# Weight casts of a projection queued behind the decays of an mLSTM head on ScalarE, in a one-layer Fox and mLSTM mixer

## The chip, the cores and the metric

The kernel runs on one core of a Trainium2 chip. The metric is the time of one execution on the device in microseconds (us); the median of several executions stands for a kernel. All data and all arithmetic are 32-bit floats; on TensorE a product of two matrices is made as three matmuls, from each operand split into a high part and a low rest.

## The reference

One layer over 256 positions of width 2048: a first feed-forward network, a token mixer, a second feed-forward network, each behind an adaptive layer norm whose nine shift, scale and gate vectors are computed from a conditioning vector. The change lies in the mixer, which is cut here to what matters:

```python
z = h @ w_in                                   # 256 x 2048 @ 2048 x 6160
y_fox = _fox_attention(fq, fk, fv, fox_logf)   # 8 heads of 128
mq, mk = ...                                   # causal convolution and silu, 4 heads of 128
hm = _mlstm(mq, mk, mv, m_i, m_logf)           # 4 heads, values of 256
...
y = jnp.concatenate([y_fox, y_mlstm], axis=-1)
return y @ w_out
```

An mLSTM head is, in the kernel's closed form over all 256 positions, a matrix of products q k, weighted by a decay exp(-max(0, ...)) below the diagonal, times the values, divided by a bounded row sum.

## The kernel before, in words

Weights come from HBM in blocks of 1 MB (tile `raw`, three buffers, one DMA each on SP's queue). For each block `load_w` lets ScalarE make the high parts `hi` (two casts of 128x1024, L150) and VectorE the low rests `lo` (two subtractions, L151), six buffers each. TensorE then runs the three matmuls of `mm3` (L399 to L401): `hi` with the high input, `hi` with the low input, `lo` with the high input.

The projections for the Fox heads are made by `form_a_four`, four blocks of 512 rows each. In the order of the program they are named `fb` (queries of heads 4 to 7), `fbk` (their keys), `fa` and `fak` (heads 0 to 3); `fbk00` and `fbk01` are the two halves of block 0 of `fbk`, and so on. Each block is 48 matmuls. After each block `step()` does two things: it pumps rows of the conditioning projection (`ar`, 512 KB rows of `w_ada` with two buffers, added into `acc` by VectorE at L165), and it advances the side work, which is Python generators of heads.

An mLSTM head (`mlstm_head`) is such a generator. Its first part makes on TensorE the row of decays `gb` and the products `sps` and `gb`; on ScalarE a Relu (L1306) and an Exp (L1307) write the decays `dm`; VectorE masks them (L1308) and multiplies them with the products (L1309). `sps` has a single PSUM buffer (tag `m5`), so the products of the next head can be written only when L1309 has read those of this one. Its second part makes `nps` on TensorE (L1315 to L1317), the divisor `dn` on VectorE (L1320 to L1323), the quotient `yM` and its squares on ScalarE (L1324, L1325). The PSUM tiles `gb` and `nps` share three buffers (tag `aux`).

A scheduler sets the order on each engine when the program is built; every engine then runs its own queue strictly in that order and waits on semaphores. `tc.issue_after(ins)` adds no wait: it orders the instructions of its block behind `ins` on the engine of `ins`.

## Time and profile before

| what | us |
|---|---|
| median of 3 runs | 1928.33 |
| lowest and highest run | 1928.22, 1933.65 |
| the profiled execution's own time | 1927.28 |
| its span | 1925.6 |
| TensorE busy in it | 1891.5 |
| ScalarE busy in it | 953.7 |
| VectorE busy in it | 1483.4 |

The span is the time between the first and the last instruction of the profile; the 1.7 us between it and the execution's own time are start and end. TensorE's matmuls are pipelined, so its busy time says that it has work, not that it runs at its peak; its idle time and its granted clock are what can be won. PE is TensorE, DVE is VectorE, ACT is ScalarE, SP issues DMAs.

### The profile page before, as it was taken

How to read it: one execution, taken by the hardware profiler on the slowest of the kernel's cores; microseconds unless marked ns; L12 is line 12 of the kernel's file. 1: busy time of each engine (PE TensorE's matmuls, PEld its weight loads, DVE VectorE, ACT ScalarE, POOL GpSimd, SP SyncE). 2: the span in 40 equal slices, each digit the busy share in tenths (PEclk: the TensorE clock that was granted, in tenths of full speed). 3: DMA queues.
4: the chain of work that ended last, by engine and by line, in shares of the span. 5: the costliest groups of instructions: out<-in, count | busy, mean ns of one | idle time of the engine just before them, and what ended most of it. 6: DMA issues, size and time to landing. Idle time of an engine off the chain costs nothing.

```text
span 1925.6 us, 32413 instructions
## 1 busy us (share of the span) xinstructions
PE 1891.5 (98%) x13133; PEld 1724.6 (90%) x13133; DVE 1483.4 (77%) x1847; ACT 953.7 (50%) x1359; POOL 59.7 (3%) x88
## 2 busy tenths in 40 slices
PE   6999999999999999999999999999999999999997
PEld 3999999999988887699989886999999999988886
DVE  6788989877789898888988887867766655555776
ACT  3554454444454555845655645565444444444562
POOL 1111100000000000100000000000000000000000
PEclk9999999999999999999999999999999999999999
DMA  9978969999898787499988883987777766755552
GB/s 359 375 262 313 328 218 296 337 331 306 266 339 296 267 301 236 138 321 317 319 300 272 315 300 114 338 282 246 262 248 260 246 213 196 240 184 189 196 196 89
DMA packets 283662, 510.92 MB, mean 265 GB/s; under 512 B 10962, under 2 KB 134514, under 8 KB 282488
## 3 DMA queue, kind: packets, MB, share of 16 engines
q1 hardware_dynamic: 275640, 480.53, 73.4%
q0 software_dynamic: 7872, 28.32, 4.4%
q8 instruction: 103, 1.69, 0.4%
q14 instruction: 47, 0.39, 0.1%
HBM read 506.71 MB, written 2.10 MB: 264 GB/s over the span
## 4 chain that ended last, share of the span: by engine, by line
PE 84%; DVE 7%; DMA 5%; issue 2%; ACT 1%; SPq 0%; DVEq 0%; POOL 0%; ACTq 0%
PE gu_f L401 8%; PE gu_f L400 8%; PE gu_f L399 8%; PE o_f L399 6%; PE o_f L401 6%; PE o_f L400 6%; PE s L400 4%; PE s L399 4%; PE s L401 4%; DMA ar<-in_w_ada_dram 3%; PE fs L401 1%; PE fs L399 1%; PE fs L400 1%; PE o_mx L399 1%; PE o_mx L401 1%
## 5 line engine op out<-in xcount | busy, mean ns | idle before, releaser
L165 DVE SCALAR_TENSOR_TENSOR acc<-ar,csil,acc 128x1024 f32<-128x1024 f32 (+1 forms) x167 | 211.4, 1267 | 52.2 <-DMA ar<-in_w_ada_dram 51.5
L400 PE MATMUL s<-xlo_f,hi_s 128*128 128x256 f32 x768 | 213.6, 278 | 1.2 <-DVE xlo_f L331 1.2
L399 PE MATMUL s<-xhi_f,hi_s 128*128 128x256 f32 x768 | 213.4, 279 | 0.0
L401 PE MATMUL s<-xhi_f,lo_s 128*128 128x256 f32 x768 | 213.3, 278 | 0.0
L401 PE MATMUL gu_f<-xhi_f,lo_f2i 128*128 128x256 f32 x768 | 212.0, 276 | 0.0
L399 PE MATMUL gu_f<-xhi_f,hi_f2i 128*128 128x256 f32 x768 | 212.0, 276 | 0.0
L400 PE MATMUL gu_f<-xlo_f,hi_f2i 128*128 128x256 f32 x768 | 212.0, 276 | 0.0
L151 DVE TENSOR_TENSOR lo_f2i<-raw_f2i,hi_f2i 128x1024 fp32r<-128x1024 f32 x96 | 117.4, 1224 | 92.4 <-ACT hi_f2i L150 92.4
L401 PE MATMUL gu_f<-xhi_f,lo_f1i 128*128 128x256 f32 x640 | 176.7, 276 | 0.0
L399 PE MATMUL gu_f<-xhi_f,hi_f1i 128*128 128x256 f32 x640 | 176.7, 276 | 0.0
L400 PE MATMUL gu_f<-xlo_f,hi_f1i 128*128 128x256 f32 x640 | 176.7, 276 | 0.0
L150 ACT CAST hi_f2i<-raw_f2i 128x1024 fp32r<-128x1024 f32 x96 | 100.8, 1050 | 135.4 <-PE gu_f L400 124.6
L150 ACT CAST hi_s<-raw_s 128x1024 fp32r<-128x1024 f32 x96 | 100.6, 1052 | 130.3 <-PE s L400 93.4
L400 PEld LDWEIGHTS s<-xlo_f,hi_s 128*128 128x128 f32 x768 | 145.5, 189 | 1.5 <-DVE xlo_f L331 1.5
L401 PEld LDWEIGHTS s<-xhi_f,lo_s 128*128 128x128 f32 x768 | 145.4, 189 | 0.0
L399 PEld LDWEIGHTS s<-xhi_f,hi_s 128*128 128x128 f32 x768 | 144.9, 189 | 0.0
L399 PEld LDWEIGHTS gu_f<-xhi_f,hi_f2i 128*128 128x128 f32 x768 | 144.2, 188 | 0.2
L400 PEld LDWEIGHTS gu_f<-xlo_f,hi_f2i 128*128 128x128 f32 x768 | 144.2, 188 | 0.2
L401 PEld LDWEIGHTS gu_f<-xhi_f,lo_f2i 128*128 128x128 f32 x768 | 144.2, 188 | 0.0
L151 DVE TENSOR_TENSOR lo_f2o<-raw_f2o,hi_f2o 128x1024 fp32r<-128x1024 f32 x86 | 105.2, 1223 | 43.3 <-ACT hi_f2o L150 43.3
L165 DVE SCALAR_TENSOR_TENSOR gate<-ar,csil,gate 128x1024 f32<-128x1024 f32 (+1 forms) x94 | 117.5, 1251 | 25.4 <-DMA ar<-in_w_ada_dram 25.2
L151 DVE TENSOR_TENSOR lo_s<-raw_s,hi_s 128x1024 fp32r<-128x1024 f32 x96 | 115.5, 1219 | 27.4 <-ACT hi_s L150 27.2
(478 smaller groups left out, 5511.6 us busy)
## 6 DMA issues: line engine op xcount, KB each, us to landing
ar<-in_w_ada_dram SPq DMA_DIRECT2D x227, 512.0 KB, 5.4
raw_f2i<-in_ffn_w_in_dram SPq DMA_DIRECT2D x48, 1024.0 KB, 5.2
raw_s<-in_ffn_w_in_dram SPq DMA_DIRECT2D x47, 1024.0 KB, 7.6
raw_f1o<-in_ffn_w_out_dram SPq DMA_DIRECT2D x44, 1024.0 KB, 7.3
raw_f2o<-in_ffn_w_out_dram SPq DMA_DIRECT2D x44, 1024.0 KB, 5.1
raw_f1i<-in_ffn_w_in_dram SPq DMA_DIRECT2D x40, 1024.0 KB, 7.4
ar<-in_w_ada_dram POOLq DMA_DIRECT2D x48, 512.0 KB, 6.9
raw_mxo<-in_w_out_dram SPq DMA_DIRECT2D x16, 1024.0 KB, 6.0
```

The lines of the kernel that those rows point to most:

```text
L150: S.copy(hi, src)
L151: return V.tensor_tensor(out=lo, in0=src, in1=hi.bitcast(F32), op=ALU.subtract)
L165: V.scalar_tensor_tensor(out=acc, in0=raw, scalar=csil[:, k:k + 1], in1=acc, op0=ALU.mult, op1=ALU.add)
L399: PE.matmul(o, ah, bh, start=start, stop=False)
L400: PE.matmul(o, ah, bl, start=False, stop=False)
L401: PE.matmul(o, al, bh, start=False, stop=stop)
```

## The change

`mlstm_head` keeps its last Exp instruction in a two-place list `decays`. `form_a_four` hands the older place to `load_w` as `behind`, and shifts the list after each block and before its `step()`. So the two casts of a weight block are ordered on ScalarE behind the decays of the head whose first part was issued after the block two before. Head 0 is issued after block 2 of `fb`, head 1 after block 3 of `fb`, head 2 after block 0 of `fbk`, head 3 after block 2 of `fbk`; the blocks bound by the order are 0, 1 and 2 of `fbk` and 0 of `fa`. No instruction is added that computes anything, and TensorE's order stays as it was.

```diff
     emptied = [None]
+    decays = [None, None]
...
-            for k4, hi, lo in load_w(W[u * 512:(u + 1) * 512, c0:c0 + 512], 4, 512, f"{name}{u}"):
+            for k4, hi, lo in load_w(W[u * 512:(u + 1) * 512, c0:c0 + 512], 4, 512, f"{name}{u}",
+                                     behind=decays[0]):
...
+            decays[:] = decays[1], None
             step()
...
-            S.activation(d, d, AF.Exp, scale=-1.0)
+            decays[1] = S.activation(d, d, AF.Exp, scale=-1.0).ins
```

The scheduler places everything around these casts anew. The first place is ScalarE's queue (ACT) at head 0. `hi_fbk..` are the casts, `dm0` the decays of head 0, `qs4` a scaled copy of finished queries. Before:

```order
L150 CAST hi_fbk00_10448<-raw_fbk0_10446 128x1024
L150 CAST hi_fbk01_10476<-raw_fbk0_10446 128x1024
L150 CAST hi_fbk10_10540<-raw_fbk1_10538 128x1024
L150 CAST hi_fbk11_10568<-raw_fbk1_10538 128x1024
L1306 ACTIVATE dm0_10354<-gb0_10352,nacol_8749 128x256
L1306 ACTIVATE dm0_10354<-gb0_10352,nacol_8749 128x128
L1307 ACTIVATE dm0_10354<-dm0_10354 128x256
L1307 ACTIVATE dm0_10354<-dm0_10354 128x128
```

In the changed kernel, whose lines lie three further down, the same place reads:

```order
L1309 ACTIVATE dm0_10354<-gb0_10352,nacol_8749 128x256
L1309 ACTIVATE dm0_10354<-gb0_10352,nacol_8749 128x128
L1310 ACTIVATE dm0_10354<-dm0_10354 128x256
L1310 ACTIVATE dm0_10354<-dm0_10354 128x128
L150 CAST hi_fbk00_10448<-raw_fbk0_10446 128x1024
L150 CAST hi_fbk01_10476<-raw_fbk0_10446 128x1024
L1386 ACTIVATE qs4_10711<-pr_fb0_10121 128x256
```

The decays of head 0 stood behind four casts and now stand ahead of them; the casts of block 1 have moved further back, behind the decays of head 1.

The second place is VectorE's queue (DVE) from the same point on: `lo_fbk..` are the low rests, `acc` takes a row `ar` of the conditioning projection, `dg` and `scsh` finish one of its vectors. Before:

```order
L151 TENSOR_TENSOR lo_fbk00_10449<-raw_fbk0_10446,hi_fbk00_10448 128x1024
L165 SCALAR_TENSOR_TENSOR acc5_0_10041<-ar5_0_8_10427,csil_94,acc5_0_10041 128x1024
L151 TENSOR_TENSOR lo_fbk01_10477<-raw_fbk0_10446,hi_fbk01_10476 128x1024
L151 TENSOR_TENSOR lo_fbk10_10541<-raw_fbk1_10538,hi_fbk10_10540 128x1024
L195 TENSOR_TENSOR dg6_1_1_10335<-bc6_1_1_10332,ident_79 128x512
L151 TENSOR_TENSOR lo_fbk11_10569<-raw_fbk1_10538,hi_fbk11_10568 128x1024
L197 TENSOR_REDUCE scsh_103<-dg6_1_1_10335 128x4
L1308 TENSOR_TENSOR dm0_10354<-dm0_10354,trir_87 128x128
L199 TENSOR_TENSOR scsh_103<-scsh_103,bcol_98 128x2x4
L1308 TENSOR_TENSOR dm0_10354<-dm0_10354,trir_87 128x128
L1309 TENSOR_TENSOR dm0_10354<-sps0_10353,dm0_10354 128x256
L1309 TENSOR_TENSOR dm0_10354<-gb0_10352,dm0_10354 128x128
```

In the changed kernel:

```order
L165 SCALAR_TENSOR_TENSOR acc5_0_10041<-ar5_0_8_10427,csil_94,acc5_0_10041 128x1024
L195 TENSOR_TENSOR dg6_1_1_10335<-bc6_1_1_10332,ident_79 128x512
L197 TENSOR_REDUCE scsh_103<-dg6_1_1_10335 128x4
L199 TENSOR_TENSOR scsh_103<-scsh_103,bcol_98 128x2x4
L1311 TENSOR_TENSOR dm0_10354<-dm0_10354,trir_87 128x128 x2
L1312 TENSOR_TENSOR dm0_10354<-sps0_10353,dm0_10354 128x256
L1312 TENSOR_TENSOR dm0_10354<-gb0_10352,dm0_10354 128x128
L151 TENSOR_TENSOR lo_fbk00_10449<-raw_fbk0_10446,hi_fbk00_10448 128x1024
L151 TENSOR_TENSOR lo_fbk01_10477<-raw_fbk0_10446,hi_fbk01_10476 128x1024
```

The four low rests of blocks 0 and 1 have moved from ahead of head 0's products to behind them; the row `ar5_0_8` and the end of the conditioning vector stay ahead.

The third place is VectorE at the low rests of block 2 of `fbk`, with head 0's divisor `dn0.` and head 2's decays. Before:

```order
L165 SCALAR_TENSOR_TENSOR acc5_0_10041<-ar5_0_9_10504,csil_94,acc5_0_10041 128x1024
L151 TENSOR_TENSOR lo_fbk20_10622<-raw_fbk2_10619,hi_fbk20_10621 128x1024
L165 SCALAR_TENSOR_TENSOR acc5_0_10041<-ar5_0_10_10596,csil_94,acc5_0_10041 128x1024
L151 TENSOR_TENSOR lo_fbk21_10650<-raw_fbk2_10619,hi_fbk21_10649 128x1024
L1308 TENSOR_TENSOR dm1_10432<-dm1_10432,trir_87 128x128 x2
L1309 TENSOR_TENSOR dm1_10432<-sps1_10431,dm1_10432 128x256
L1309 TENSOR_TENSOR dm1_10432<-gb1_10430,dm1_10432 128x128
L165 SCALAR_TENSOR_TENSOR acc5_0_10041<-ar5_0_11_10599,csil_94,acc5_0_10041 128x1024
L151 TENSOR_TENSOR lo_fbk30_10722<-raw_fbk3_10719,hi_fbk30_10721 128x1024
L165 SCALAR_TENSOR_TENSOR acc5_0_10041<-ar5_0_12_10677,csil_94,acc5_0_10041 128x1024
L1320 SCALAR_TENSOR_TENSOR dn00_10512<-nps00_10507,em_8750 128x1
```

In the changed kernel:

```order
L165 SCALAR_TENSOR_TENSOR acc5_0_10041<-ar5_0_10_10596,csil_94,acc5_0_10041 128x1024
L165 SCALAR_TENSOR_TENSOR acc5_0_10041<-ar5_0_11_10599,csil_94,acc5_0_10041 128x1024
L1323 SCALAR_TENSOR_TENSOR dn00_10512<-nps00_10507,em_8750 128x1
L1323 SCALAR_TENSOR_TENSOR dn01_10518<-nps01_10508,em_8750 128x1
L1325 TENSOR_TENSOR dn00_10512<-nps00_10507,dn00_10512 128x1
L1325 TENSOR_TENSOR dn01_10518<-nps01_10508,dn01_10518 128x1
L1326 RECIPROCAL dn00_10512<-dn00_10512 128x1
L1326 RECIPROCAL dn01_10518<-dn01_10518 128x1
L1311 TENSOR_TENSOR dm2_10526<-dm2_10526,trir_87 128x128 x2
L1312 TENSOR_TENSOR dm2_10526<-sps2_10525,dm2_10526 128x256
L1312 TENSOR_TENSOR dm2_10526<-gb2_10524,dm2_10526 128x128
L151 TENSOR_TENSOR lo_fbk20_10622<-raw_fbk2_10619,hi_fbk20_10621 128x1024
```

The low rest of block 2 now follows the divisor of head 0 and the decays of head 2, and all of them follow row 11 of the conditioning projection. On ScalarE the quotients `yM0` and their squares stand ahead of head 2's Relu and Exp, and those ahead of the casts of block 2. On SP's queue the DMA of row 11 now stands ahead of that of block 0 of `fa`, and not behind it.

## Prediction

> **What bounds the kernel now.** I read the page first (busy shares), then TensorE's list of waits, then the stretches around the longest wait, then the timelines of the four queues there.

> ```profile
> PE 1891.5 (98%) x13133; PEld 1724.6 (90%) x13133; DVE 1483.4 (77%) x1847; ACT 953.7 (50%) x1359; POOL 59.7 (3%) x88
> PE sps L1303 <- DVE dm L1309: 4.1, 1, 4.1
> 800.00:900.00 100.00, 99.15 (x624) 88.52 (x623) 82.59 (x125) 59.14 (x105) 2.30 (x6) 1.00 0.92 317
> 970.00:980.00 10.00, 5.90 (x36) 5.65 (x35) 10.00 (x18) 4.19 (x9) 0.00 (x0) 0.83 0.97 337
> 980.00:990.00 10.00, 10.00 (x83) 9.75 (x81) 7.34 (x15) 5.89 (x15) 0.00 (x0) 1.00 0.93 318
> ```

> TensorE is the bound: it is busy 98% of the span. The second row is its wait (total, times, longest) that the change touches: the products of head 1 wait once, 4.1 us, for VectorE. The stretches give busy time by engine, then the granted clock: around the wait it falls to 0.83, ten us later it is 1.00. Time won there is won at the end, since TensorE stays the bound behind it.

> ```profile
> 963.83 0.59 PE L1303 MATMUL sps<-o 128*128 128x256 f32 x2
> 964.40 0.37 PE L399 MATMUL pr_fb<-xhi_mx,hi_fb 128*128 128x256 f32 x1
> 969.98 0.28 PE L1301 MATMUL gb<-ng,rowsel 128*128 128x256 f32 x1
> 974.36 0.70 PE L1303 MATMUL sps<-o 128*128 128x256 f32 x2 [4.10 <-DVE dm L1309]
> 982.22 1.03 PE L1315 MATMUL nps<-yM,dm 128*128 128x257 f32 x4
> 984.22 0.37 PE L399 MATMUL pr_fbk<-xhi_mx,hi_fbk 128*128 128x256 f32 x1
> 989.78 1.03 PE L1315 MATMUL nps<-yM,dm 128*128 128x257 f32 x4
> 990.89 0.47 PE L399 MATMUL pr_fbk<-xhi_mx,hi_fbk 128*128 128x256 f32 x1
> 996.56 1.03 PE L1315 MATMUL nps<-yM,dm 128*128 128x257 f32 x4
> 997.99 0.38 PE L1301 MATMUL gb<-ng,rowsel 128*128 128x256 f32 x1
> ```

> On TensorE (start, duration) head 0's products run from 963.83 to 964.40 (0.57 us), and a block at full clock takes 989.78 - 984.22 = 5.56. From head 1's products to nps of head 0 the same two pieces take 982.22 - 974.36 = 7.86, so 7.86 - 6.13 = 1.73 is lost to the lower clock behind the wait. The spot costs 4.10 + 1.73 = 5.83 us.

> **The change part by part.** ScalarE and VectorE before, at head 0:

> ```profile
> 962.38 2.00 ACT L150 CAST hi_fbk<-raw_fbk 128x1024 fp32r<-128x1024 f32 x2
> 966.32 2.00 ACT L150 CAST hi_fbk<-raw_fbk 128x1024 fp32r<-128x1024 f32 x2 [1.94 <-DMA raw_fbk<-in_w_in_dram]
> 968.23 0.72 ACT L1306 ACTIVATE dm<-gb,nacol 128x256 f32<-128x256 f32 x2
> 968.84 0.61 ACT L1307 ACTIVATE dm<-dm 128x256 f32<-128x256 f32 x2
> 965.71 1.22 DVE L151 TENSOR_TENSOR lo_fbk<-raw_fbk,hi_fbk 128x1024 fp32r<-128x1024 f32 x1
> 967.61 1.28 DVE L165 SCALAR_TENSOR_TENSOR acc<-ar,csil,acc 128x1024 f32<-128x1024 f32 x1 [0.69 <-DMA ar<-in_w_ada_dram]
> 968.81 2.35 DVE L151 TENSOR_TENSOR lo_fbk<-raw_fbk,hi_fbk 128x1024 fp32r<-128x1024 f32 x2
> 971.08 0.68 DVE L195 TENSOR_TENSOR dg<-bc,ident 128x512 f32<-128x512 f32 x1
> 971.68 1.21 DVE L151 TENSOR_TENSOR lo_fbk<-raw_fbk,hi_fbk 128x1024 fp32r<-128x1024 f32 x1
> 973.89 0.41 DVE L1309 TENSOR_TENSOR dm<-sps,dm 128x256 f32<-128x256 f32 x1
> 974.23 0.28 DVE L1309 TENSOR_TENSOR dm<-gb,dm 128x128 f32<-128x128 f32 x1
> ```

> Starts follow each other a little faster than the durations say: a low rest 1.14 (a pair 2.27), a row of `acc` 1.20, dg 0.60; I use these steps.

> *Head 0, what goes.* The Relu stood behind casts of block 1, whose weights landed only at 966.32, and ran at 968.23. It now runs when gb is there, about 964.7, and the Exp ends near 966; then VectorE sets the end. It still takes row 8 when it lands, 967.61, so dg at 968.81, the reduce at 969.41, scsh at 970.0, the two masks from 970.1 and the product with sps at about 970.5, to 970.9. TensorE asks for the buffer at 969.98 + 0.28 = 970.26. A wait of 0.71 is left, to 970.97.

> *Low rest of block 0, what is late next.* It starts behind the products, at 971.03, and ends at 972.25. TensorE reaches it two matmuls into the block, about 971.77: 0.48 more. The block ends at 972.02 + 5.56 = 977.58, where nps stood at 982.22 before. The two casts of block 0 (965.9 to about 967.8) are ready in time.

> *Block 2, the new chain.* Here the added order puts work in front of weights. Rows for it, from the same heads before, and SP's queue:

> ```profile
> 975.72 2.67 SPq L184 DMA_DIRECT2D ar<-in_w_ada_dram  x2
> 981.38 1.28 DVE L165 SCALAR_TENSOR_TENSOR acc<-ar,csil,acc 128x1024 f32<-128x1024 f32 x1 [1.28 <-DMA ar<-in_w_ada_dram]
> 979.08 0.48 DVE L1308 TENSOR_TENSOR dm<-dm,trir 128x128 f32<-128x128 f32 x2
> 979.49 0.41 DVE L1309 TENSOR_TENSOR dm<-sps,dm 128x256 f32<-128x256 f32 x1
> 991.51 0.16 DVE L1322 TENSOR_TENSOR dn<-nps,dn 128x1 f32<-128x1 f32 x1
> 991.71 0.16 DVE L1323 RECIPROCAL dn<-dn 128x1 f32<-128x1 f32 x1
> 986.50 0.84 ACT L1324 ACTIVATE yM<-nps,dn 128x256 f32<-128x256 f32 x2 [1.27 <-DVE dn L1323]
> 988.02 0.61 ACT L1307 ACTIVATE dm<-dm 128x256 f32<-128x256 f32 x2
> 991.96 0.47 ACT L1324 ACTIVATE yM<-nps,dn 128x256 f32<-128x256 f32 x1 [1.05 <-DVE dn L1323]
> 992.79 0.19 ACT L1325 ACTIVATION_READ_ACCUMULATOR nps<-yM 128x1 f32 x1
> ```

> VectorE: after the second low rest of block 0 (972.2 to 973.3) come row 9 (to 974.5), head 1's decays (0.95, to 975.45), both low rests of block 1 (to 977.7) and row 10 (to 978.9). Row 11 can be fetched when row 9 has freed its buffer, 974.6; row 11 took 981.38 - 975.72 = 5.66 from issue to use before, so it is there at about 980.2, and VectorE stands for 1.3 us. With 1.20 for the row, head 0's divisor starts at 981.4 and takes two dependent steps of 0.2 and some 0.15 more: 981.9. On ScalarE two quotients with their squares take 988.02 - 986.50 = 1.52: 983.45. Relu and Exp follow in steps of 0.61 and 0.5, so the cast of fbk20 starts at 984.6 and ends at 985.6; head 2's masks and products on VectorE, 0.95, end at about 985.7. The low rest then runs to 986.9. TensorE, running nps and products as before in 984.22 - 982.22 = 2.00, is through block 1 at 977.58 + 2.00 + 5.56 = 985.14, through nps of head 1 (990.89 - 989.78 = 1.11) at 986.25, and needs that rest at 986.48: a wait of 0.45. Block 2 ends at 992.26.

> *Head 1's squares.* PSUM for the products of head 3 is free when head 1's second square is done. VectorE: second rest of block 2 to 988.0, row 12 to 989.2, the two rests of block 3 with head 1's divisor between them to 991.8, row 13 to 993.0, last reciprocal 993.2. ScalarE needs 992.79 + 0.19 - 991.96 = 1.02 for quotient and square: 994.3. TensorE would be there at 992.26 + 1.11 = 993.37: a wait of 0.93. Head 3's row gb then starts at 994.3 and not at 997.99.

> *Behind it.* The casts of block 0 of `fa` stand behind head 3's decays. ScalarE has from 994.3 some 3.6 us of quotients, squares, Relu and Exp, cast to about 999.0, rest to 1000.2; TensorE needs it at 994.3 + 0.79 (997.99 to 998.78 before) + 5.56 + 0.23 = 1000.9. Covered by 0.7; were that gone, each us would be lost in full. Since the rests free the buffers of `raw`, blocks are also fetched later:

> ```profile
> 979.19 0.38 SPq L374 DMA_DIRECT2D raw_fa<-in_w_in_dram  x1
> raw_fa<-in_w_in_dram SPq DMA_DIRECT2D x4, 1024.0 KB, 7.6
> ```

> Block 1 of `fa` went out at 979.19, when block 2 of `fbk` was done with; now it goes at 988.0, nine us later. With the 7.6 us of such a block to landing it is there at 995.6, ahead of its cast near 1000. That costs nothing until it lands 4 us late. SP's row 11, now ahead of block 0 of `fa`, has one block less in front of it.

> *The sum.* Gone 5.83, and 0.43 of small waits between 990 and 998 (block 2 took 5.67 against 5.56; gb came 1.43 and not 1.11 behind nps). Added 0.71 + 0.48 + 0.45 + 0.93 = 2.57. Net 3.69, the same as 997.99 - 994.3. The profiled execution took 1927.28, so 1923.6 by its own clock; its span starts and ends in the same overhead, and the median of the runs lies 1.05 above it. I forecast the median: 1928.33 - 3.7 = 1924.6. The unknown is the row landing; bounds are below.

> *The clock.* The stretch 800 to 900 holds 0.85 us of TensorE's idle time at a granted clock of 1.00, so waits under a us cost only themselves here. [...] The sum goes by the row.

> **The rivals.**

> *Clean.* Row 8 and row 11 each land a us sooner, so that neither wait forms: up to 5.83 + 0.43 = 6.26 is won, 1922.1, just over the 0.3% (5.8 us) that a measurement of this kernel can tell from no change. For it: DMA is 0.97 busy there and rows vary. Against: the low rest of block 0 stays late in any case. Chance 0.13.

> *The clock falls for small waits.* Two falls at 1.73 give back 3.46: 1928.1. Against it the 800 to 900 stretch; for it that four waits lie closer here. [...]

> *Row 11 blocks VectorE.* Head 0's divisor, head 2's decays and block 2's weights now all stand behind one DMA.

> ```profile
> 1283.91 8.94 DMA ar<-in_w_ada_dram
> ```

> A row has taken 8.94 elsewhere on the chain that ended last. Then all is 8.94 - 5.66 = 3.3 later, the wait at block 2 grows to 3.7 and lowers the clock for another 1.73: 3.69 - 3.3 - 1.73 = -1.3, so 1929.6, slower than before. With the clock lowered it decides from a landing of 5.66 + 3.69 - 1.73 = 7.6 on. Chance 0.10; slower by 0.3% needs 13 us or more.

> *The wait stays.* The order binds ScalarE alone; if row 8 lands 3.4 later, head 0's products are as late as before: 1928.3. Chance 0.07, since nothing but the order of rows has changed ahead of it.

> **How the numbers follow.** The forecast has 0.56 (0.04 is kept for what I overlooked) and its own range is 1922.8 (only the 0.71 left, 5.55 won) to 1926.3 (2 won). The range of 8 in 10 runs from the clean case, 1922.0, to the blocked row, 1929.6. Faster by over 0.3%: 0.13 from the clean case. Slower by over 0.3%: what I overlooked, 0.04, and a row of 13 us or a second blocked one, 0.04 of the 0.10, together 0.08. Within 0.3%: 0.79.

> **What would show it.** Right: TensorE's wait at sps falls from 4.1 to under 1; the stretch behind it holds a clock near 1.00; short waits appear at the low rests of `fbk` and at head 3's gb; VectorE idles for a DMA of `ar` ahead of L1323; block 0 of `fa` starts 3 to 4 us earlier. Wrong: a wait over 2 us anywhere between 980 and 1010, a second stretch of low clock, or a gain there that is gone before the end.

## The result, and the profile after

The changed kernel takes 1925.72 us at the median (1921.45 to 1931.05, 22 runs), the kernel before beside it 1929.36 us (1926.21 to 1935.96, 22 runs). The ratio is 0.9979, with a 95% interval of 0.9971 to 0.9986: some 4.0 us are won (2.7 to 5.6). The forecast was 1924.6 and 3.7 us won, and a change within 0.3%, which it is. The profiled execution of the changed kernel took 1929.01 us (span 1927.3), longer than its median; some 3.4 us of that (half of 6.83) come from two windows at half clock at 240 us (shown at the end); by its mean granted clock, 0.996 against 0.993 here, the second profile of the same kernel (e1) seems to have none such.

These rows of after answer to those of before: the page's busy row, TensorE's waits, and two stretches (busy time by engine, then granted clock, DMA share, GB/s). PEld is TensorE's loading of weights; of a wait the row gives total, times, longest.

```profile
PE 1895.2 (98%) x13133; PEld 1728.3 (90%) x13133; DVE 1482.0 (77%) x1847; ACT 950.8 (49%) x1359; POOL 60.7 (3%) x88
PE sps L1306 <- DVE dm L1312: 1.9, 1, 1.9
970.00:980.00 10.00, 7.90 (x54) 7.44 (x53) 8.13 (x16) 5.02 (x10) 0.00 (x0) 0.86 0.73 237
980.00:990.00 10.00, 10.00 (x80) 9.78 (x80) 6.41 (x15) 3.59 (x11) 0.00 (x0) 0.97 0.97 355
```

The wait at head 1's products is 1.9 us where it was 4.1, and the clock behind it still falls (0.86 and 0.97). The timelines of the four queues say why:

```profile
966.17 0.34 SPq L184 DMA_DIRECT2D ar<-in_w_ada_dram  x1
967.14 0.29 PE L1304 MATMUL gb<-ng,rowsel 128*128 128x256 f32 x1
967.26 0.60 PE L1306 MATMUL sps<-o 128*128 128x256 f32 x2
968.12 0.73 ACT L1309 ACTIVATE dm<-gb,nacol 128x256 f32<-128x256 f32 x2 [1.34 <-PE gb L1306]
972.01 1.28 DVE L165 SCALAR_TENSOR_TENSOR acc<-ar,csil,acc 128x1024 f32<-128x1024 f32 x1 [1.80 <-DMA ar<-in_w_ada_dram]
975.14 0.41 DVE L1312 TENSOR_TENSOR dm<-sps,dm 128x256 f32<-128x256 f32 x1
975.61 0.70 PE L1306 MATMUL sps<-o 128*128 128x256 f32 x2 [1.93 <-DVE dm L1312]
976.94 0.39 PE L401 MATMUL pr_fbk<-xhi_mx,lo_fbk 128*128 128x256 f32 x1 [0.17 <-DVE lo_fbk L151]
999.36 0.47 PE L1304 MATMUL gb<-ng,rowsel 128*128 128x256 f32 x1
```

ScalarE does what the change says: Relu starts as soon as TensorE has written head 0's scores (1.34 us of idle time end with them). VectorE then stands 1.80 us for row 8 of `w_ada`, issued at 966.17 and taken at 972.01 (5.84 us), and only behind it come the masks and the product with sps.

A measure that does not depend on where a trace begins is the way on TensorE from head 0's gb to head 3's. In the group of gb (first and last start at the end of the row; first before, then after):

```profile
L1301 PE MATMUL gb<-ng,rowsel x4: 280/332/474, 963.7 to 998.0; 128*128 128x256 f32 x4
L1304 PE MATMUL gb<-ng,rowsel x4: 280/378/474, 967.1 to 999.4; 128*128 128x256 f32 x4
```

It is 34.3 us before and 32.2 after (963.72 to 997.99, and 967.14 to 999.36). I call it the heads' way below; every experiment but one (e7) has the same work on it. That one profile shows 2.0 of the 4.0 us; the rest is what the experiments are for.

### The profile page after: what moved, and what is told of

Same layout as the page of the kernel before. It is cut to its first block, busy times and chain, and to the rows that moved or that the text cites. A ratio compares the mean times of both kernels' runs of the same rounds, so it can differ in the third digit from the quotient of the medians.

```text
span 1927.3 us, 32400 instructions
## 1 busy us (share of the span) xinstructions
PE 1895.2 (98%) x13133; PEld 1728.3 (90%) x13133; DVE 1482.0 (77%) x1847; ACT 950.8 (49%) x1359; POOL 60.7 (3%) x88
## 4 chain that ended last, share of the span: by engine, by line
PE 88%; DMA 5%; DVE 4%; issue 1%; ACT 1%; SPq 0%; POOL 0%; DVEq 0%; ACTq 0%
PE gu_f L400 8%; PE gu_f L401 8%; PE gu_f L399 8%; PE o_f L399 8%; PE o_f L401 8%; PE o_f L400 8%; PE s L400 4%; PE s L399 4%; PE s L401 4%; DMA ar<-in_w_ada_dram 2%; PE fs L401 1%; PE fs L400 1%; PE fs L399 1%; PE o_mx L399 1%; PE o_mx L401 1%; PE o_mx L400 1%
## 5 line engine op out<-in xcount | busy, mean ns | idle before, releaser
L165 DVE SCALAR_TENSOR_TENSOR acc<-ar,csil,acc 128x1024 f32<-128x1024 f32 (+1 forms) x167 | 211.4, 1267 | 63.1 <-DMA ar<-in_w_ada_dram 62.2
L399 PE MATMUL s<-xhi_f,hi_s 128*128 128x256 f32 x768 | 214.4, 280 | 0.0
L399 PE MATMUL gu_f<-xhi_f,hi_f2i 128*128 128x256 f32 x768 | 212.0, 276 | 0.0
L151 DVE TENSOR_TENSOR lo_f2i<-raw_f2i,hi_f2i 128x1024 fp32r<-128x1024 f32 x96 | 117.4, 1224 | 93.2 <-ACT hi_f2i L150 93.2
L399 PE MATMUL gu_f<-xhi_f,hi_f1i 128*128 128x256 f32 x640 | 176.7, 276 | 0.0
L150 ACT CAST hi_f2i<-raw_f2i 128x1024 fp32r<-128x1024 f32 x96 | 100.8, 1050 | 135.4 <-PE gu_f L400 124.6
L150 ACT CAST hi_s<-raw_s 128x1024 fp32r<-128x1024 f32 x96 | 100.5, 1052 | 132.7 <-PE s L400 90.0
L399 PEld LDWEIGHTS s<-xhi_f,hi_s 128*128 128x128 f32 x768 | 146.1, 191 | 0.0
L399 PEld LDWEIGHTS gu_f<-xhi_f,hi_f2i 128*128 128x128 f32 x768 | 144.1, 188 | 0.2
L165 DVE SCALAR_TENSOR_TENSOR gate<-ar,csil,gate 128x1024 f32<-128x1024 f32 (+1 forms) x94 | 117.4, 1250 | 27.4 <-DMA ar<-in_w_ada_dram 27.2
L151 DVE TENSOR_TENSOR lo_f2o<-raw_f2o,hi_f2o 128x1024 fp32r<-128x1024 f32 x86 | 105.2, 1223 | 43.3 <-ACT hi_f2o L150 43.3
L151 DVE TENSOR_TENSOR lo_s<-raw_s,hi_s 128x1024 fp32r<-128x1024 f32 x96 | 115.5, 1219 | 27.1 <-ACT hi_s L150 27.0
## 6 DMA issues: line engine op xcount, KB each, us to landing
raw_f2i<-in_ffn_w_in_dram SPq DMA_DIRECT2D x48, 1024.0 KB, 5.1
raw_s<-in_ffn_w_in_dram SPq DMA_DIRECT2D x47, 1024.0 KB, 7.5
raw_f1o<-in_ffn_w_out_dram SPq DMA_DIRECT2D x44, 1024.0 KB, 7.3
raw_f2o<-in_ffn_w_out_dram SPq DMA_DIRECT2D x44, 1024.0 KB, 5.0
raw_f1i<-in_ffn_w_in_dram SPq DMA_DIRECT2D x40, 1024.0 KB, 7.9
raw_mxo<-in_w_out_dram SPq DMA_DIRECT2D x16, 1024.0 KB, 7.5
```

The source lines that it names most:

```text
L150: S.copy(hi, src)
L151: return V.tensor_tensor(out=lo, in0=src, in1=hi.bitcast(F32), op=ALU.subtract)
L165: V.scalar_tensor_tensor(out=acc, in0=raw, scalar=csil[:, k:k + 1], in1=acc, op0=ALU.mult, op1=ALU.add)
L399: PE.matmul(o, ah, bh, start=start, stop=False)
```

## The experiments

My theory after the result: the gain is the meeting of TensorE with head 0's products, and what keeps it from being larger is row 8, which stands ahead of those products on VectorE and is taken whenever its DMA lands. Rivals: the orders of the other heads matter on their own; the single PSUM buffer is the cause, whoever fills it; or the kernel's engines are simply full here and a wait removed comes back elsewhere.

**The change once more (e1), no edit.**

> The changed kernel once more, for a second profile. Theory A (the gain is the wait of head 1's products sps and the low clock behind it, and what is left of that wait is set by the landing of conditioning row 8 ahead of head 0's products on VectorE): the wait at sps is not the same again; it is between 0.3 and 2.5 us and ends 3.3 us after VectorE starts row 8. The time is 2 to 5 us under the kernel before. Theory B (the gain comes from the changed order of DMAs and rows, and the wait at sps only moves): the time gained does not go with the wait at sps.

1925.5 us (12 runs), ratio 0.9976 (0.9965 to 0.9988). In this profile row 8 was there in time:

```profile
964.62 0.34 SPq L184 DMA_DIRECT2D ar<-in_w_ada_dram  x1
965.59 0.28 PE L1304 MATMUL gb<-ng,rowsel 128*128 128x256 f32 x1
967.39 2.60 DVE L165 SCALAR_TENSOR_TENSOR acc<-ar,csil,acc 128x1024 f32<-128x1024 f32 x2
972.30 0.70 PE L1306 MATMUL sps<-o 128*128 128x256 f32 x2 [0.20 <-DVE dm L1312]
973.63 0.38 PE L401 MATMUL pr_fbk<-xhi_mx,lo_fbk 128*128 128x256 f32 x1 [0.17 <-DVE lo_fbk L151]
988.17 0.39 PE L401 MATMUL pr_fbk<-xhi_mx,lo_fbk 128*128 128x256 f32 x1
995.47 0.39 PE L1304 MATMUL gb<-ng,rowsel 128*128 128x256 f32 x1 [0.18 <-ACT nps L1328]
970.00:980.00 10.00, 9.62 (x76) 9.06 (x75) 9.93 (x17) 3.79 (x8) 0.00 (x0) 1.00 0.87 326
```

Rows 7 and 8 run back to back from 967.39 to 969.99, and one takes 1.28, so row 8 was begun at 968.7, 4.1 us behind its issue, against 5.84 in the other execution. The wait at sps is 0.20, the clock stays at 1.00, and the heads' way is 29.9 us, 4.4 less than before. Row 8 was issued 0.97 us ahead of head 0's gb in both profiles, and the program is the same; on the queues ahead of head 0's products the landing of that row is the difference that I find. (Ahead of the heads there is another wait, for a low rest of `fb`. It is none before, 1.4 us in e9, 0.3 in the profile after, 1.1 here, and so comes and goes between executions of one kernel; the heads' way leaves it out.)

**Head 0's order alone (e2).** In the changed kernel:

```
-            decays[1] = S.activation(d, d, AF.Exp, scale=-1.0).ins
+            e = S.activation(d, d, AF.Exp, scale=-1.0).ins
+            if h == 0:
+                decays[1] = e
```

> Only the casts of block 0 of fbk are queued behind head 0's decays; those of heads 1 to 3 are free as before. Theory A: the wait at sps is as in the changed kernel (0.7 to 2 us by the landing of row 8), and the new chain at block 2 is gone, so the gain is as large or up to 1 us larger: 3.5 to 5 us. Theory B: with one of four orders left, the gain is 1 us or less.

1928.65 us (12 runs), ratio 0.9988 (0.9975 to 1.0): about half the gain, against my expectation, though the interval reaches from no gain to all of it. The profiled execution, 1932.46 us, was the slowest of the twelve. TensorE's longest wait among its heads, and two rows of VectorE:

```profile
PE gb L1304 <- ACT nps L1330: 2.7, 1, 2.7
999.62 1.28 DVE L165 SCALAR_TENSOR_TENSOR acc<-ar,csil,acc 128x1024 f32<-128x1024 f32 x1 [2.13 <-DMA ar<-in_w_ada_dram]
1000.82 0.15 DVE L1328 RECIPROCAL dn<-dn 128x1 f32<-128x1 f32 x1
```

A row that stands between the steps of head 1's divisor lands late (VectorE stands 2.13 us for it), and the reciprocal, the square behind it and head 3's gb wait for it. It is the same cause at another place: a row of `w_ada` at the head of VectorE's queue. The changed kernel has one row between these steps (992.96 in e1, with no wait), this one and the kernel before have two. So this profile shows how a late row costs; what the orders of heads 1 to 3 are worth on their own it does not show.

**The orders of heads 1 to 3 alone (e3).** As e2 with `if h > 0:`.

> The change's casts stand behind the decays of heads 1 to 3 only; head 0's casts are ordered as before the change. Theory (the time comes from head 0's Relu and Exp running ahead of the later casts, so that VectorE has the products for head 1's sps early; the orders of heads 1 to 3 only keep that gain): the wait at head 1's sps stays, 2 to 4.5 us, with a half-clock window of about 3.4 us behind it, and the median is within 0.1% of before (ratio 0.999 to 1.001). Rival (the gain lies in head 1's squares and head 3's gb, which came late by 2.7 us in the run with head 0's order alone): ratio 0.998 or lower although the wait at head 1's sps stands.

1929.18 us (11 runs), ratio 1.0 (0.999 to 1.0009), as the theory had it in time, but not in its reason:

```profile
PE sps L1306 <- DVE dm L1314: 6.0, 1, 6.0
965.51 0.61 ACT L1310 ACTIVATE dm<-dm 128x256 f32<-128x256 f32 x2
973.79 1.28 DVE L165 SCALAR_TENSOR_TENSOR acc<-ar,csil,acc 128x1024 f32<-128x1024 f32 x1 [2.45 <-DMA ar<-in_w_ada_dram]
975.47 0.42 DVE L1314 TENSOR_TENSOR dm<-sps,dm 128x256 f32<-128x256 f32 x1
```

Exp was done at 966.1, 2.6 us behind head 0's gb and so nearly as early as in the changed kernel (2.2), since here only two casts stand ahead of it. The product ran at 975.47, because VectorE's queue had rows 8 and 9 in front, and row 9 landed at 973.79. An early Exp alone won nothing here; the wait was decided on VectorE. Since head 0's Exp came early all the same, this run does not single out the orders of heads 1 to 3 either, and what they are worth stays open.

**Two heads' sps in one tile (e4).** In the kernel before:

```
-        sps = [fifth_tile(f"sps{h}")[:, :T], gb[:, T:T + P]]
+        if h % 2 == 0:
+            twin[0] = fifth_tile(f"sps{h}")
+        sps = [twin[0][:, h % 2 * T:(h % 2 + 1) * T], gb[:, T:T + P]]
```

> The kernel before, with the products sps of two heads side by side in one PSUM bank (256 of 512 columns each), so that head 1's products need not wait until VectorE has read head 0's; no order of casts is added. Theory A: the wait of 4.1 us at sps and the stretch of half clock behind it are gone; 5 to 5.8 us are gained, 0.26 to 0.30%. Theory B: the wait reappears at the next thing that needs head 0's decays (nps of head 0, some 6 us on), or nothing is gained: under 1.5 us.

1929.66 us (12 runs), ratio 0.9995 (0.9982 to 1.0009). The wait did not go:

```profile
PE sps L1306 <- DVE dm L1312: 4.5, 1, 4.5
```

As built, TensorE still waits for VectorE's product of head 0 before it writes head 1's half of that tile. So this run tells only that the time stays where the wait stays; a second tile was not tried, and whether it would end the wait is open.

**The change, and the rows behind the products (e5).** The pumped rows of `w_ada` are put on VectorE behind whatever `pin` holds; one more entry puts them behind a head's last product:

```
-            V.tensor_tensor(out=d, in0=sps[i], in1=d, op=ALU.mult)
+            pin["d"] = V.tensor_tensor(out=d, in0=sps[i], in1=d, op=ALU.mult).ins
```

> The changed kernel, and the conditioning rows pumped after a head are also queued on VectorE behind that head's products, so row 7 and row 8 no longer stand ahead of head 0's. Theory A: head 0's products end near 967 and the wait at sps is gone (under 0.4 us), whatever row 8 does; no low clock; 1 to 3 us faster than the changed kernel, 5 us under the kernel before. Theory B: as the changed kernel, and the rows moved back cost time later.

1922.8 us (6 runs), ratio 0.9959 (0.9943 to 0.9975).

```profile
968.90 0.42 DVE L1312 TENSOR_TENSOR dm<-sps,dm 128x256 f32<-128x256 f32 x1
969.43 1.27 DVE L165 SCALAR_TENSOR_TENSOR acc<-ar,csil,acc 128x1024 f32<-128x1024 f32 x1
971.52 0.60 PE L1306 MATMUL sps<-o 128*128 128x256 f32 x2
993.35 0.70 PE L1318 MATMUL nps<-yM,dm 128*128 128x257 f32 x2 [0.76 <-ACT nps L1328]
```

Row 7 (969.43) and with it row 8 now run behind the product, which is done 2.2 us before TensorE asks for the buffer; sps has no wait, and the clock stays at 1.00. Timed beside the change, four of its six runs lie under the fastest of e1's twelve (1923.44).

**The rows alone (e6).** The same line in the kernel before, without the order of the casts.

> The kernel before, with no order between casts and decays, but conditioning rows of w_ada that are pumped later are queued on VectorE behind a head's last product. Theory (two things stand ahead of head 0's products, ScalarE's casts ahead of its Relu and Exp, and row 8 ahead of the products on VectorE; each alone keeps the wait): the wait at head 1's sps shrinks by at most the time that row 8 takes (1.3 to 2.6 us) and stays at 1.5 to 3 us with a half-clock window behind it; ratio 0.998 to 1.000. Rival (row 8 alone holds the products): the wait is under 0.8 us, the clock stays at 1.00 there, and the ratio is 0.996 as with both.

1925.55 us (12 runs), ratio 0.9987 (0.9978 to 0.9997).

```profile
PE sps L1303 <- DVE dm L1309: 2.5, 1, 2.5
972.30 0.42 DVE L1309 TENSOR_TENSOR dm<-sps,dm 128x256 f32<-128x256 f32 x1
```

As the theory had it: 2.5 us of wait and a fall of the clock are left, since casts still hold up Relu and Exp. Against before the ratios are 0.9987 for the rows alone, 0.9976 for the casts alone (e1) and 0.9959 for both: 1.3 and 2.4 thousandths make 3.7, and 4.1 were measured, well within the intervals. So each order helps without the other, and both win more than one. That the two parts simply add is not shown: each interval is some 2 thousandths wide, and by the medians of e6 (1925.55 and 1929.51 beside it) the rows alone win 2.1.

**Heads 1 and 2 a block later (e7).** In the kernel before:

```
-        if h % 2:
+        for _ in range((0, 2, 1, 1)[h]):
             yield True
```

> The kernel before, without any order of the casts, but heads 1 and 2 are issued one block of the fbk product later, so that head 1's sps come some 5.5 us later on TensorE while head 0's decays and products stay where they were. Theory (only the meeting of TensorE with head 0's late products costs time, 4.1 us of wait and 1.7 us of half clock): the wait at head 1's sps goes to under 0.5 us with no half-clock window there, and the median falls by 3 to 6 us unless head 3's gb, which is now nearer to head 2, waits in its place: ratio 0.997 to 0.999. Rival (the cost is ScalarE's and VectorE's load in these blocks, which is only shifted): the wait turns up one block later, 2 to 4 us at head 1's or head 2's sps or at a low rest of fbk, ratio 0.9995 to 1.001.

1932.06 us (12 runs), ratio 1.0015 (1.0003 to 1.0026): slower, and the rival's picture.

```profile
PE gb L1301 <- DVE dm L1309: 4.0, 1, 4.0
PE pr_fb L401 <- DVE lo_fb L151: 2.4, 1, 2.4
989.02 0.42 DVE L1309 TENSOR_TENSOR dm<-sps,dm 128x256 f32<-128x256 f32 x1
```

The 4 us turn up a block later, at head 2's gb, behind head 1's product at 989.02, which is late for the same reasons: casts that waited 3.52 us for their weights stand ahead of its Relu, and two rows ahead of its masks. Moving the one who waits won nothing while the queues he waits for kept their order. (The 2.4 us at a low rest of `fb` are the wait ahead of the heads.)

**The kernel before once more (e9), no edit.**

> The kernel before once more, for a second profile of it. Theory: the wait at head 1's sps is again 3.5 to 5 us, with at least one half-clock window of 3.4 us behind it, whatever row 8's landing, since ScalarE's casts stand ahead of head 0's Exp in every execution. Rival (the wait hangs on the landing of the w_ada rows alone): it differs from 4.1 us by over 1.5 us where row 8 lands at another time.

1929.09 us in its one run.

```profile
PE sps L1303 <- DVE dm L1309: 4.5, 1, 4.5
964.76 0.34 SPq L184 DMA_DIRECT2D ar<-in_w_ada_dram  x1
970.00 1.28 DVE L165 SCALAR_TENSOR_TENSOR acc<-ar,csil,acc 128x1024 f32<-128x1024 f32 x1
L1301 PE MATMUL gb<-ng,rowsel x4: 280/336/474, 965.7 to 1000.4; 128*128 128x256 f32 x4
```

Row 8, issued at 964.76, ran at 970.00 with no wait of note for its DMA, and sps still waited 4.5 us; the heads' way is 34.7. Before the change the wait is there without a late row.

**Both once more (e8), and rows behind the divisors too (e10).** e8 is e5 unchanged. In e10 also:

```
-            V.reciprocal(dn[:, 1:2], dn[:, 0:1])
+            pin["d"] = V.reciprocal(dn[:, 1:2], dn[:, 0:1]).ins
```

> The change and the rows behind the products, the same kernel as e5_rows_behind, once more for a second profile and more timed runs. Theory (casts and rows each hold part of the 4.1 us, and with both out of the way nothing waits long enough at head 1's sps to lower the clock, wherever the rows land): no wait over 0.5 us at head 1's sps, clock 1.00 from 965 to 990 us, ratio 0.994 to 0.998. Rival (its lead over the change alone is the luck of early rows in one profile): ratio 0.9965 to 0.999, like the change alone.

> As e8_both_again, and rows pumped later also stand behind the reciprocals of a head's divisors on VectorE, because row 12 stood inside head 1's divisors and the squares behind them held up TensorE by 0.76 us at an nps. Theory: that 0.76 us goes, it was a wait of its own and too short for the clock, so the median falls by under 1 us against e8_both_again, ratio 0.9935 to 0.997. Rival (rows that stand behind still more work come late, and the next stage's conditioning waits for them): as slow as e8_both_again or slower by up to 2 us, with a new wait at a bc or a row of the stage behind.

e8: 1920.79 us (6 runs), ratio 0.9959 (0.9944 to 0.9974). e10: 1920.0 us (6 runs), ratio 0.9958 (0.9941 to 0.9975). Of e8, TensorE and the stretch:

```profile
970.00:980.00 10.00, 10.00 (x83) 9.78 (x82) 7.63 (x19) 6.81 (x16) 0.00 (x0) 1.00 0.89 309
961.33 0.28 PE L1304 MATMUL gb<-ng,rowsel 128*128 128x256 f32 x1
967.72 0.60 PE L1306 MATMUL sps<-o 128*128 128x256 f32 x2
968.61 0.28 PE L401 MATMUL pr_fbk<-xhi_mx,lo_fbk 128*128 128x256 f32 x1
982.95 0.28 PE L401 MATMUL pr_fbk<-xhi_mx,lo_fbk 128*128 128x256 f32 x1
989.30 0.47 PE L1304 MATMUL gb<-ng,rowsel 128*128 128x256 f32 x1
```

No wait is left among the heads, and their way is 28.0 us. e10 has 27.9 and cannot be told from e8: in e8 there was no 0.76 us to win. The interval of e8 meets that of the change (0.9971 to 0.9986) only at its edge. By the ratios e5 and e8 win 7.9 us (5 to 11), more than the 6.3 that the heads' way became shorter; the interval holds 6.3, and whether there is more to it is open. As for the rivals: a wait removed here did not come back among the heads, and with the single PSUM buffer left as it is the wait is gone, so the buffer alone does not make it; whether a second buffer would end it too was not tried. e8 is the smaller edit.

## Why the prediction was right, step by step

The execution e8 has no wait on the heads' way, so the differences of the other executions from it price each term, also where the trace lists less (at block 0 e1 lists 0.17 us, and the way is 0.44 longer there).

| from, to on TensorE | e8 | e1 | e1 more | predicted | profile after more |
|---|---|---|---|---|---|
| head 0's gb to head 1's sps | 6.39 | 6.71 | 0.32 | 0.71 | 2.08 |
| to the first low rest, block 0 | 0.89 | 1.33 | 0.44 | 0.48 | 0.44 |
| to the first low rest, block 2 | 14.34 | 14.54 | 0.20 | 0.45 | with the next, |
| to head 3's gb | 6.35 | 7.30 | 0.95 | 0.93 | 1.73 |
| sum | 27.97 | 29.88 | 1.91 | 2.57 | 4.25 |

*The spot's price* was right: 5.83 plus 0.43 of small waits, 6.26; the heads' way went from 34.3 to 28.0 us when nothing waited, 6.3. That is also the price of the rival *Clean*, which the change alone did not reach (e1 came to 1.9 us from it) and which the change with the rows did: the way of e8.

*Head 0's Relu and Exp* start with the scores, as said. But the step "then VectorE sets the end" carried more than I gave it: e3 has a nearly as early Exp and a wait of 6.0 us.

*The wait left at sps* is the term that was mis-sized: 0.71 predicted, 0.20 listed in e1 and 1.93 in the profile after, around the value I took, because the row's landing is no constant. The issue of row 8 on SP's queue before:

```profile
961.75 0.34 SPq L184 DMA_DIRECT2D ar<-in_w_ada_dram  x1
```

From issue to use it took 5.86 us there (967.61), 5.84 in the profile after, and 4.1 in e1. In the profile after, row 8 was also issued nearer to head 0's products, 1.1 us ahead of them (966.17 and 967.26) where it had been 2.1 (961.75 and 963.83). That is not the change's doing: in e9, the kernel before once more, it was 1.1 too (964.76 and 965.85). So the predicted time for row 8 rested on an execution that issued it early.

*Low rest of block 0*: 0.44 in both executions, against 0.48. *Block 2, the new chain*: 0.20 in e1 against 0.45. *Head 1's squares*: 0.95 in e1 against 0.93. In the profile after, the lower clock swallowed these last two: TensorE was late itself.

*The clock.* The sum took it that a wait under a us costs only itself. That held (0.20 in e1, 0.76 in e5: 1.00 behind both), and it held for several of them: through e1's four short delays (0.20 to 0.95 us in the table) the clock stayed at 1.00, from 965 to 998 us. At 1.93 us it did not hold, and 1.7 us were lost behind it (half of 3.41 us at 0.50), once and not twice. So the rival *The clock falls for small waits*, to which I gave a chance of 0.10, had half its mechanism in that one execution, for a wait that was not small; the 4.0 us of the timed runs lie nearer to e1's 4.4 than to that execution's 2.0. *The wait stays* came in part: in the profile after VectorE stood 1.80 us for row 8, and 1.93 of the 4.1 us of wait were left. *Row 11 blocks VectorE* was not seen (VectorE stood 1.0 us for that row in e1, 1.3 predicted), though e2 shows its mechanism with another row (2.13 us, and head 3's gb 2.7 us late).

*Where the net came out*: 3.69 predicted; 4.4 us on the heads' way in e1, 2.0 in the profile after, and 4.0 (2.7 to 5.6) by the runs. By the prediction's own signs the profile after failed two, the wait at sps under 1 and the clock near 1.00 behind it, and e1 met both. The mechanism was right, and the number was in part luck: it lies between two executions of one kernel, too low for one and too high for the other, by a term that it took for a constant.

## What to carry to other kernels

When an engine waits for a product, follow every queue that feeds it, each to its own head: here ScalarE's casts and VectorE's rows each held the same product, and an order on one queue alone left the other to decide. A step that waits for a DMA does not belong ahead of the work that the bounding engine is about to ask for; put behind it, in e5 and e8, the rows no longer held it up. Judge a change of a few us by several profiles and by the distance between two fixed matmuls, since one execution can show half the gain.

## What the runs showed of the hardware

```profile
971.59:975.00 3.41, 0.64 (x3) 0.59 (x4) 3.41 (x9) 1.63 (x3) 0.00 (x0) 1.00 0.98 364
```

```profile
973.80:977.21 3.41, 1.44 (x8) 1.18 (x9) 3.34 (x9) 0.65 (x3) 0.00 (x0) 1.00 0.82 302
977.21:980.62 3.41, 3.41 (x18) 3.41 (x18) 3.41 (x7) 2.76 (x6) 0.00 (x0) 0.50 0.40 94
236.52:239.93 3.41, 2.50 (x23) 2.30 (x22) 3.41 (x8) 1.25 (x3) 0.00 (x0) 1.00 0.72 222
239.93:243.34 3.41, 3.41 (x19) 3.41 (x18) 2.04 (x6) 2.70 (x7) 0.00 (x0) 0.50 0.49 190
```

```profile
961.04:964.45 3.41, 1.77 (x15) 1.77 (x16) 3.41 (x7) 3.04 (x7) 0.00 (x0) 1.00 0.91 318
964.45:967.87 3.42, 3.08 (x23) 2.66 (x22) 3.42 (x4) 3.39 (x5) 0.55 (x1) 1.00 1.02 354
```

A window with 0.64 or 1.44 us of work is followed by one at half clock; one with 1.77 is not, although e7's wait of 2.4 us, shared between two windows, is longer than the 1.93 that fell almost wholly into one. Of the windows cut at the grid around the heads (before, after, e2, e5, e6, e7), each of the six at full clock with up to 1.44 us of work was followed by a fall (0.64, 0.86, 0.98, 1.13, 1.39, 1.44), and none of the six with 1.77 to 2.69 (1.77, 2.08, 2.26, 2.32, 2.65, 2.69). The clock was back at 1.00 behind a window at half that was full of work (3.41 us, before and after); behind one with 1.98, in e7, it stayed at half for another:

```profile
988.35:991.76 3.41, 1.98 (x7) 1.83 (x8) 1.90 (x9) 3.14 (x9) 0.00 (x0) 0.50 0.83 282
991.76:995.17 3.41, 3.41 (x18) 3.41 (x17) 3.41 (x6) 2.06 (x6) 0.00 (x0) 0.50 0.99 361
```

In e2 the falls begin at 964.61 and 1002.16, which is 11 windows apart; in the profile after, at 239.93 and 977.21, 216 windows. So, as an estimate from these windows, a single wait under some 1.6 us (3.41 less 1.77) costs itself, and one of 2 to 3 us costs 1.7 more (half of 3.41) or not by where the grid lies, as 1.93 us did in the profile after and 2.4 in e7 did not; that can be part of why the runs of one kernel spread by several us.

One case speaks against a plain threshold: in the profile after, at 236.52, a window with 2.50 us of work was followed by two at half clock. The first of the two was full of work (3.41 us), and still the second came (243.34 to 246.76, at 0.50). The start of the kernel does not fit either: in the profile before, a window with 1.89 us of work (29.49 to 32.91) was followed by one at full clock with 2.75, and only then by two at half clock (36.32 to 43.14). Nothing in these runs tells why, and it stays open.
